# Row maximum on one core: the last rows' pieces cut at multiples of 64 columns, and GpSimd's 38 blocks taken from five loads instead of four

## The chip, the core and the metric

The kernel runs on one core of one Trainium2 chip. The metric is the device time of one execution in microseconds (us). The kernel before has a median of 163.62 us over three timed runs (163.60, 163.62 and 163.85).

The core has several engines that work side by side and wait for each other through semaphores. DVE (VectorE) does the reductions here, PE (TensorE) transposes, ACT (ScalarE) copies PSUM to SBUF, POOL (GpSimd) takes a maximum across partitions, and SP (SyncE) issues the loads. PSUM is the memory that TensorE writes to; SBUF is the main on-chip memory of 128 partitions.

## The reference

```python
def setup_inputs():
    batch, seq, dim = 32, 512, 1024
    return {"x": np.random.randn(batch, seq, dim).astype(np.float32)}

def reference(x):
    return np.max(x, axis=-1).astype(np.float32)
```

There are 32 x 512 = 16384 rows of 1024 float32, so 64 MiB are read and 64 KiB written. Each partition holds 128 rows.

## The kernel before

**Loads.** `BLOCKS` gives the sizes of 18 loads, numbered 0 to 17, in rows per partition: 2, 15, 16, 14, 11, 11, 10, 10, 8, 8, 7, 3, 3, 3, 2, 1, 1, 1. They go into a ring of 47 rows per partition, all from SP's queue (L238). The last two rows of each partition come after them in four smaller transfers, the pieces (L243): `PIECES` holds the widths. `issue()` sends a load as soon as the program has put down the readers of what the load overwrites.

**The plan.** `PLAN` is written out by hand, and `in_turn` keeps each engine's instructions in its order. Its steps are:

- `dN` (`direct`): DVE reduces those rows of load N that it alone handles, into the result columns.
- `tN` (`turn`): GpSimd's share, chunk N. TensorE transposes 128x128 blocks into PSUM (L160), ScalarE copies them to SBUF (L166), GpSimd takes the maximum over the 128 partitions (L168), so one transposed block's row maxima end up side by side in one partition.
- `bN` (`back`): TensorE turns that chunk's results back into a column per block, one small matmul for each block (L178), written into a PSUM tile.
- `pN` (`partial`): where GpSimd has only a part of a row's eight blocks, DVE reduces the rest of the row into a column of the same PSUM tile.
- `mN` (`merge`): DVE reduces the columns of that PSUM tile into the result. `m10` does load 10's tile, called `got`; `m99` does the tile `joint`, which the loads of `RANK` have in common.
- `fN`: DVE reduces piece N. The second piece of a row takes the first one's maximum along as one more column.

**GpSimd's share.** `SHARED = {load: (rows, blocks of each row)}` gives GpSimd 3 rows x 8 blocks of load 10, 2 x 3 of load 13, 2 x 3 of load 14 and 1 x 2 of load 17: 38 blocks in chunks of 8, 8, 8, 6, 6 and 2, which are t0 to t5. The three whole rows of load 10 need nothing of DVE but `m10`.

**What sets the order at the end.** The plan ends `... b1 d13 t3 p13 b2 p14 t4 m10 d15 b3 d16 p17 t5 f0 b4 f1 f2 b5 f3 m99`. A DVE instruction that writes `joint` waits for the TensorE writes to `joint` ahead of it in the plan, and the other way round, since both engines write to one tile. Thus in the kernel before `p17` waits for `b3`, and `b4` waits for `p17`. A DVE write to `joint` also waits for the DVE write to `joint` just ahead of it. The pools `turned` (ACT's copies) and `allr` (GpSimd's results) have two buffers each, so a chunk reuses the buffers of the chunk two ahead of it: GpSimd may write chunk k's result once `b(k-2)` has read the earlier one.

**The end.** Two stores carry the result out from ScalarE's queue: the first block's 112 columns behind `f0` (L271), the second block's 16 columns behind `m99` (L273).

Of the kernel before, what the change touches and what calls it, by code (L numbers as in the profile page):

```python
# [8 lines left out]
F32 = mybir.dt.float32  # L9

BLOCKS = [
    [2, 15, 16, 14, 11, 11, 10, 10, 8, 8, 7],
    [3, 3, 3, 2, 1, 1, 1],
# [1 line left out]
RING = 47  # L17


SHARED = {10: (3, 8), 13: (2, 3), 14: (2, 3), 17: (1, 2)}  # L20

RANK = {13: 1, 14: 2, 17: 2}

PIECES = [(532, 492), (592, 432)]

PLAN = """
    d0 d1 d2 d3 d4 d5 d6 d7 d8 d9 t0 d10 t1 t2 d11 b0 d12 b1 d13 t3 p13 b2 p14 t4 m10 d15 b3
    d16 p17 t5 f0 b4 f1 f2 b5 f3 m99
""".split()

NOSYNC = mybir.DependencyInfo(mybir.DependencyClass.NoSync, mybir.DependencyReason.DATA)
# [4 lines left out]
def kernel(  # L41
# [11 lines left out]
    N, D = xf.shape  # L53
    C = D // P
    I = N // P
# [10 lines left out]
    ring = once.tile([P, I + RING * D], F32)  # L66
    res = ring[:, :I]
# [9 lines left out]
    def maximum(out, in_):  # L77
        return in_turn("DVE", nc.vector.reduce_max(out=out, in_=in_, axis=X))  # L78
# [15 lines left out]

    loads = []
    views = []
    last = len(PIECES)
    first = at = 0
    for sizes in BLOCKS:
        S = sum(sizes) + last * (sizes is BLOCKS[-1])  # L100
        xb = xf[first * P:(first + S) * P, :].rearrange("(p i) d -> p i d", p=P)
# [5 lines left out]
        b, place = 0, {}  # L107
        for i in sorted(range(len(sizes)), key=lambda i: RANK.get(base + i, 0)):
            place[i] = b
# [8 lines left out]
    assert first == I  # L118
    shared = [SHARED.get(j, (0, C)) for j in range(len(loads))]

    lead = [0 if RANK.get(j) == 3 else n - m for j, ((_, n, _, _), (m, _)) in enumerate(zip(loads, shared))]
    final = [j for j in range(len(loads)) if j in RANK]
    final.sort(key=lambda j: loads[j][3])
# [11 lines left out]
    def rows(j):  # L135
        start, n, _, _ = loads[j]
        return ring[:, I + start * D:I + (start + n) * D].rearrange("p (i d) -> p i d", d=D)
# [4 lines left out]
    def share(j):  # L142
        m, parts = shared[j]
        if j in RANK:
            r = loads[j][3] + lead[j] - col0
            return joint[:, r:r + m, :]
        if j not in fetched:
            got = psmall.tile([P, m, parts + (parts < C)], F32)
            fetched[j] = got
        return fetched[j]  # L150
# [39 lines left out]
    def partial(j):  # L190
        m, parts = shared[j]

        s = width - parts if j in RANK else 1
        maximum(share(j)[:, :, parts:], rows(j)[:, lead[j]:lead[j] + m, parts * P:].rearrange(
# [11 lines left out]
    pieces = []  # L206
    tail = []
    room = I + at * D
    for q in range(len(PIECES[0])):
        for r, widths in enumerate(PIECES):  # L210
            c, w = sum(widths[:q]), widths[q]
            room = -(-(room + 1) // 16) * 16
            pieces.append((ring[:, room:room + w], xb[:, S - last + r, c:c + w]))
            if q:
                tail[-last] = (ring[:, room - 1:room], tail[-last][1])
            tail.append((res[:, I - last + r:I - last + r + 1],
                         ring[:, room - (q > 0):room + w]))
            room += w
    assert room <= I + (at + last + 1) * D


# [81 lines left out]
```

## Time and profile before

| what | value |
|---|---|
| median of three timed runs | 163.62 us |
| span of the profiled execution, first to last instruction | 162.0 us |
| what lies around the span, taken as the difference of the two | 1.6 us |
| DVE busy | 135.3 us (84%), 33 instructions |
| POOL busy | 16.0 us (10%) |
| PE busy | 13.6 us (8%) |
| loads | 67.11 MB, mean 415 GB/s over the span |

The profiled execution's own time is not listed apart from the three timed runs, so its span plus 1.6 us stands for it. GpSimd works in the last 20 us of the span alone: the page's slices show POOL idle until load 10 has landed. A row of a group or of the timeline reads: start, duration, engine, line, operation, output<-input, shapes, count, and in brackets how long the engine sat idle before it and what ended that.

### The profile page before, as it was taken

What the parts mean: (1) busy time and instruction counts of PE and PEld (TensorE: products, weight loads), DVE (VectorE), ACT (ScalarE), POOL (GpSimd) and SP (SyncE); (2) the same over time, 40 slices, a digit from 0 to 9 for tenths busy, and PEclk for the clock granted to TensorE, in tenths of its full rate; (3) what the DMA queues carried; (4) which work ended last, traced back from release to release, by engine and by line L of the source; (5) the groups of instructions that cost most, each with busy time, mean ns of one, the idle gap of its engine ahead of it and who ended that gap; (6) DMA issues with size and microseconds to landing.
All of it is one profiled execution on the core that took longest, in us unless ns stands there. A gap on an engine that the chain in (4) does not pass through costs nothing.

```text
span 162.0 us, 297 instructions
## 1 busy us (share of the span) xinstructions
PE 13.6 (8%) x76; PEld 11.7 (7%) x76; DVE 135.3 (84%) x33; ACT 6.3 (4%) x7; POOL 16.0 (10%) x11
## 2 busy tenths in 40 slices
PE   0000000000000000000000000000000000772942
PEld 0000000000000000000000000000000000762731
DVE  3500019998399999999999999996999999999994
ACT  0020000000000000000000000000000000241120
POOL 0000000000000000000000000000000000099791
PEclk9999999999999999999999999999999999997555
DMA  5996999599789999898999899799999999999991
GB/s 176 569 486 273 455 502 518 259 518 518 326 354 453 453 405 534 356 534 356 434 456 455 354 486 465 344 486 388 429 478 388 424 418 453 395 431 419 412 386 47
DMA packets 3456, 67.18 MB, mean 415 GB/s; under 512 B 640, under 2 KB 896, under 8 KB 1536
## 3 DMA queue, kind: packets, MB, share of 16 engines
q1 hardware_dynamic: 3168, 67.11, 97.0%
q10 hardware_dynamic: 288, 0.07, 0.2%
HBM read 67.11 MB, written 0.07 MB: 415 GB/s over the span
## 4 chain that ended last, share of the span: by engine, by line
DMA 50%; DVE 47%; SPq 1%; issue 0%; DVEq 0%
DMA ring<-in_x_dram 50%; DVE ring L78 45%; DVE joint L78 2%; SPq L238 1%; DVEq L298 0%
## 5 line engine op out<-in xcount | busy, mean ns | idle before, releaser
L78 DVE TENSOR_REDUCE ring<-ring 128x1 f32<-128x1024 f32 (+13 forms) x20 | 130.0, 6548 | 23.4 <-DMA ring<-in_x_dram 23.3
L168 POOL PARTITION_ALL_REDUCE top<-sb x6 | 15.7, 2657 | 135.0 <-ACT sb L166 134.9
L160 PE MATMUL ps<-ident,ring 128*128 128x128 f32 x38 | 9.1, 424 | 139.9 <-DMA ring<-in_x_dram 139.9
L160 PEld LDWEIGHTS ps<-ident,ring 128*128 128x128 f32 x38 | 7.6, 224 | 139.9 <-issue 139.9
L166 ACT COPY sb<-ps 128x1024 f32<-128x1024 f32 (+2 forms) x6 | 5.0, 834 | 143.2 <-PE ps L160 136.2
L78 DVE TENSOR_REDUCE joint<-ring 128x2 f32<-128x1280 f32 (+1 forms) x3 | 3.9, 1314 | 0.0
L178 PE MATMUL got<-ident,top 1*128 1x1 f32 x24 | 2.7, 228 | 3.7 <-POOL top L168 3.6
L178 PEld LDWEIGHTS got<-ident,top 1*128 1x128 f32 x24 | 2.4, 188 | 4.6 <-POOL top L168 4.6
L178 PE MATMUL joint<-ident,top 1*128 1x1 f32 x14 | 2.0, 245 | 1.9 <-POOL top L168 1.9
L178 PEld LDWEIGHTS joint<-ident,top 1*128 1x128 f32 x14 | 1.7, 210 | 2.7 <-POOL top L168 2.7
L166 ACT ACT_TABLE_LOAD x1 | 1.3, 1283 | 7.9 <-DVE ring L78 7.9
L83 DVE MEMSET ident<- 128x128 f32 x1 | 0.2, 165 | 0.8 <-PEq L287 0.8
L255 POOL MEMSET gate<- 128x1 f32 x1 | 0.1, 99 | 7.4 <-DVE ring L78 7.4
L90 DVE TENSOR_SCALAR rowno<-rowno 32x1 f32<-32x1 f32 x3 | 0.4, 146 | 0.1
L85 DVE TENSOR_TENSOR_SCAN colno<-ident 128x128 f32<-128x128 f32 x1 | 0.4, 424 | 0.0
L92 DVE TENSOR_SCALAR ident<-colno,rowno 128x128 f32<-128x128 f32 x1 | 0.3, 288 | 0.0
L87 DVE STREAM_TRANSPOSE rowno<-colno 128x32 f32<-128x32 f32 x1 | 0.2, 213 | 0.0
L78 DVE TENSOR_REDUCE ring<-got 128x3 f32<-128x24 f32 x1 | 0.2, 173 | 0.0
L78 DVE TENSOR_REDUCE ring<-joint 128x5 f32<-128x20 f32 x1 | 0.2, 169 | 0.0
L287 POOL MEMSET const-float32-0.0<- 128x1 f32 x1 | 0.1, 98 | 0.2 <-issue 0.2
L287 POOL MEMSET const-bfloat16-1.0<- 128x1 bf16 x1 | 0.1, 101 | 0.0
L287 POOL MEMSET const-uint8-127<- 128x1 uint8 x1 | 0.1, 101 | 0.0
(2 smaller groups left out, 0.2 us busy)
## 6 DMA issues: line engine op xcount, KB each, us to landing
ring<-in_x_dram SPq DMA_DIRECT2D x2, 5632.0 KB, 29.9
ring<-in_x_dram SPq DMA_DIRECT2D x2, 5120.0 KB, 36.8
ring<-in_x_dram SPq DMA_DIRECT2D x2, 4096.0 KB, 32.5
ring<-in_x_dram SPq DMA_DIRECT2D x1, 7680.0 KB, 22.5
ring<-in_x_dram SPq DMA_DIRECT2D x1, 7168.0 KB, 57.8
ring<-in_x_dram SPq DMA_DIRECT2D x3, 1536.0 KB, 35.7
ring<-in_x_dram SPq DMA_DIRECT2D x1, 3584.0 KB, 29.2
ring<-in_x_dram SPq DMA_DIRECT2D x2, 1024.0 KB, 17.7
```

The lines of the kernel that those rows point to most:

```text
L78: return in_turn("DVE", nc.vector.reduce_max(out=out, in_=in_, axis=X))
L83: in_turn("DVE", nc.vector.memset(ident, 1.0))
L85: in_turn("DVE", nc.vector.tensor_tensor_scan(out=colno, data0=ident, data1=ident, initial=-1.0, op0=ALU.add, op1=ALU.mult))
L87: in_turn("DVE", nc.vector.transpose(out=rowno, in_=colno[:, :32]))
L90: in_turn("DVE", nc.vector.tensor_scalar(out=part, in0=part, scalar1=float(q * 32), scalar2=None, op0=ALU.add))
L92: identity = in_turn("DVE", nc.vector.tensor_scalar(out=ident, in0=colno, scalar1=rowno[:, 0:1], scalar2=None, op0=ALU.is_equal))
L160: in_turn("PE", nc.tensor.transpose(out=ps[:, w:w + P], in_=rows(j)[:, lead[j] + r + i, c * P:(c + 1) * P], identity=ident,))
L166: in_turn("ACT", nc.scalar.copy(out=sb[:, :W], in_=ps[:, :W]))
L168: in_turn("POOL", nc.gpsimd.partition_all_reduce(top[:, :W], sb[:, :W], P, bass_isa.ReduceOp.max))
L178: in_turn("PE", nc.tensor.transpose(out=share(j)[:, r + i, c:c + 1], in_=tops[k][0:1, w:w + P], identity=ident[0:1, 0:1],))
L238: load = nc.sync.dma_start(out=rows(issued), in_=src)
L287: nc = _bacc.Bacc("TRN2", target_bir_lowering=False, num_devices=1)
```

## The change

The four pieces of the last two rows become 640 and 384 columns of the one row and 576 and 448 of the other, in the same order of rows; before they were 532 and 492, and 592 and 432. Their places in the source are now multiples of 64 columns, and in the ring they start at multiples of 64 columns instead of 16.

GpSimd's 38 blocks now come from five loads: 6 rows x 4 blocks of load 10, 3 x 2 of load 13, 2 x 2 of load 14, 1 x 2 of load 16 and 1 x 2 of load 17. The chunks are 8, 8, 8, 6, 4, 2 and 2 blocks: t0 to t6, with b0 to b6. DVE takes the rest of these rows in `p10`, `p13`, `p14`, `p16` and `p17`; `d13` and `d16` are gone. `joint` has seven rows of three columns instead of five of four, and `m10` reduces 6 x 5 instead of 3 x 8. The number and the sizes of the 18 loads stay; with load 16 in `RANK`, some loads of the second block take other rows of the source.

```diff
-SHARED = {10: (3, 8), 13: (2, 3), 14: (2, 3), 17: (1, 2)}
-RANK = {13: 1, 14: 2, 17: 2}
-PIECES = [(532, 492), (592, 432)]
+SHARED = {10: (6, 4), 13: (3, 2), 14: (2, 2), 16: (1, 2), 17: (1, 2)}
+RANK = {13: 1, 14: 2, 16: 2, 17: 2}
+PIECES = [(0, 640), (1, 576), (0, 384), (1, 448)]
 PLAN = """
-    d0 d1 d2 d3 d4 d5 d6 d7 d8 d9 t0 d10 t1 t2 d11 b0 d12 b1 d13 t3 p13 b2 p14 t4 m10 d15 b3
-    d16 p17 t5 f0 b4 f1 f2 b5 f3 m99
+    d0 d1 d2 d3 d4 d5 d6 d7 d8 d9 t0 d10 p10 t1 t2 d11 b0 d12 b1 p13 t3 b2 p14 t4 m10 d15 b3
+    p16 t5 p17 t6 b4 f0 f1 b5 f2 f3 b6 m99
 """.split()
...
-    last = len(PIECES)
+    last = 1 + max(r for r, _ in PIECES)
...
-    for q in range(len(PIECES[0])):
-        for r, widths in enumerate(PIECES):
-            c, w = sum(widths[:q]), widths[q]
-            room = -(-(room + 1) // 16) * 16
-            pieces.append((ring[:, room:room + w], xb[:, S - last + r, c:c + w]))
-            if q:
-                tail[-last] = (ring[:, room - 1:room], tail[-last][1])
-            tail.append((res[:, I - last + r:I - last + r + 1],
-                         ring[:, room - (q > 0):room + w]))
-            room += w
+    done = [0] * last
+    before = [None] * last
+    for r, w in PIECES:
+        c, q = done[r], before[r]
+        room = -(-(room + 1) // 64) * 64
+        pieces.append((ring[:, room:room + w], xb[:, S - last + r, c:c + w]))
+        if q is not None:
+            tail[q] = (ring[:, room - 1:room], tail[q][1])
+        before[r] = len(tail)
+        tail.append((res[:, I - last + r:I - last + r + 1], ring[:, room - (q is not None):room + w]))
+        done[r] = c + w
+        room += w
```

More of the change, by code (lines that the diff above doesn't have):

```diff
@@ L208 @@
     room = I + at * D
-    for q in range(len(PIECES[0])):
-        for r, widths in enumerate(PIECES):
-            c, w = sum(widths[:q]), widths[q]
-            room = -(-(room + 1) // 16) * 16
-            pieces.append((ring[:, room:room + w], xb[:, S - last + r, c:c + w]))
-            if q:
-                tail[-last] = (ring[:, room - 1:room], tail[-last][1])
-            tail.append((res[:, I - last + r:I - last + r + 1],
-                         ring[:, room - (q > 0):room + w]))
-            room += w
+    done = [0] * last
[10 more added lines that the diff above has]
+        room += w
+    assert done == [D] * last
     assert room <= I + (at + last + 1) * D
```

## The prediction

> **What bounds the kernel now.** I read the waits first, then the chain that ended last, then the timeline of the last 13 us, engine by engine in short windows so that single instructions show. The waits of DVE, in the rows of the page by shape:
>
> ```profile
> L78 DVE TENSOR_REDUCE ring<-ring 128x15 f32<-128x15360 f32 x1 | 16.2, 16155 | 15.8 <-DMA ring<-in_x_dram 15.8
> L78 DVE TENSOR_REDUCE ring<-ring 128x16 f32<-128x16384 f32 x1 | 17.2, 17222 | 3.2 <-DMA ring<-in_x_dram 3.2
> L78 DVE TENSOR_REDUCE ring<-ring 128x10 f32<-128x10240 f32 x2 | 21.6, 10821 | 1.3 <-DMA ring<-in_x_dram 1.3
> ```
>
> These are DVE's large waits, all for loads, the last ahead of the second 10-row load at 110.82 us. From there DVE has no large gap. The loads come at one pace to the end: issue time plus time to landing in the view of DMA issues gives 149.81 (load 13), 152.3 (14), 154.85 (16), 156.1 (17), and 158.9 for the last piece (149.82 + 9.1). So near the end loads and DVE run level: load 13 lands at 149.81 and DVE, just done with load 12, starts on it at 149.83. The chain in order of time, from there:
>
> ```profile
> 149.83 1.22 DVE ring L78
> 151.05 1.41 DVE joint L78
> 152.46 0.02 issue
> 152.48 1.50 DVE joint L78
> 153.98 2.23 DVE ring L78 x3
> 156.21 0.04 issue
> 156.26 0.96 DVE joint L78
> 157.22 1.16 DVE ring L78 x2
> ...
> 159.00 0.59 DVE ring L78
> ```
>
> Everything here is DVE; whatever it waits for in this stretch moves the end one to one. Now TensorE and GpSimd beside it:
>
> ```profile
> 149.94 1.51 PE L160 MATMUL ps<-ident,ring 128*128 128x128 f32 x6 [0.55 <-DMA ring<-in_x_dram]
> 154.99 0.79 PE L178 MATMUL joint<-ident,top 1*128 1x1 f32 x6 [0.92 <-POOL top L168]
> 157.61 0.79 PE L178 MATMUL joint<-ident,top 1*128 1x1 f32 x6 [0.68 <-POOL top L168]
> 158.66 0.37 PE L178 MATMUL joint<-ident,top 1*128 1x1 f32 x2 [0.25 <-POOL top L168]
> 148.23 3.30 POOL L168 PARTITION_ALL_REDUCE top<-sb  x1
> 152.43 2.50 POOL L168 PARTITION_ALL_REDUCE top<-sb  x1 [0.90 <-ACT sb L166]
> 157.49 1.12 POOL L168 PARTITION_ALL_REDUCE top<-sb  x1
> ```
>
> The second row is `b3`: it begins 0.05 after `t3`'s all-reduce (152.43 to 154.94) and ends at 155.78. In the kernel before only `p17` waits for it, and `p17` starts at 156.26 for load 17's sake. So `b3` is 0.48 us early and shows in no wait. The last small matmuls end at 159.03, 0.48 ahead of `m99` at 159.51.
>
> **Part 1, load 10: no cost.** One reduction of 4096 columns (4.41 us) becomes `d10` of 1024 and `p10` of 3072. A 1024 row takes 1.21 and a 3072 row 3.34, but consecutive reductions overlap: 3072 to 3072 is 146.44 - 143.18 = 3.26 from start to start, 1024 to 1024 is 155.10 - 153.98 = 1.12, and 4096 is 143.18 - 138.85 = 4.33. So the new pair costs 1.12 + 3.26 - 4.33 = 0.05. `p10` reads with a stride and writes to PSUM; the nearest rows (1280 columns, two strided rows to PSUM, 1.48 against 1.33 at 0.96 columns/ns) show the same fixed 0.15 as the contiguous ones, so bounds are -0.05 (no extra) and +0.1. Its cover is the slack at 149.83: load 12's reduction could have been followed at 149.70 and waited for load 13. If that cover is gone, the rest falls into the stall of part 3. TensorE's first three chunks have 24 blocks as before, start with load 10's landing (138.7) as before, and GpSimd's first three all-reduces end at 151.53 as before. `b0` now waits for `p10` too, which ends near 143.3, while `b0` waits for GpSimd until 145.18. `m10` over 30 columns instead of 24: 6 columns, 0.01.
>
> **Part 2, loads 13 to 15.** Before, DVE goes 149.83 to 155.10 with `d13`, `p13`, `p14`, `m10` and `d15`. After: `p13` has 3 x 768 = 2304 columns, 2.40 + 0.15 = 2.55, to 152.38; `p14` waits for its predecessor (0.03, as 152.45 to 152.48 now), 1536 columns, 1.60 + 0.16 = 1.76, to 154.18; `m10` and `d15` follow at the old distances (153.89, 153.98 against `p14`'s end 153.98), so `d15` starts at 154.18 and DVE could go on at 154.18 + 1.12 = 155.30. Against 155.10 that is 0.20 more, for the 256 columns more that lie ahead of this point (the `d16` and `p17` before are 1792 columns, `p16` and `p17` after 1536). The total of columns from load 13 on is equal.
>
> **Part 3, the wait that decides.** `p16` writes `joint` and stands behind `b3` in the plan. In the built program it waits for TensorE's 64th counted matmul: 24 of t0 to t2, 24 of b0 to b2, 6 of t3, 4 of t4, 6 of b3. `b3` does not move: `t3` has six blocks as before, starts from load 13's landing, copies at 151.54, reduces at 152.43, and `b3`'s six matmuls again end at 155.78. (`b3` also waits for `p14`, at 154.18, before GpSimd is done.) TensorE to another engine costs 0.03 to 0.09 (copies: 140.77 to 140.80; 151.45 to 151.54); I take 0.05, since `p16`'s other waits are over by then. So `p16` starts at 155.83, not at 155.30: a stall of 0.53. Behind it on DVE stand `p17`, all four pieces and `m99`, and nothing hides it.
>
> **Part 4, from `p16` to the end on DVE.** `p16` is 768 columns, 0.96; `p17` waits for its end (0.03): 156.82. Then, by the old start-to-start distances and 1/0.96 ns a column: `p17` to `f0` 0.86 (156.26 to 157.12), 157.68; `f0` 0.62 + 108 columns (0.11), 158.41; `f1` 0.68 - 0.02, 159.07; `f2` 0.58 - 0.11, 159.54; `f3` 0.51 + 0.02, so `m99` could start at 160.07. The pieces themselves have landed: the bytes are the same, the last lands near 158.9, and `f3` starts 0.65 later. Their alignment is therefore worth nothing here, whatever it does to a transfer.
>
> **Part 5, the new last round of GpSimd.** `t6` uses `t4`'s result buffer, so it waits for `b4`, which stands behind `t6` on TensorE and waits for `p17` (the last DVE write to `joint`), done at 157.78. `b4` starts 0.05 (GpSimd to TensorE, 154.94 to 154.99) to 0.13 (landing to TensorE, 149.81 to 149.94) later: 157.87. Four matmuls, between two (0.37) and six (0.79): 0.58, to 158.45. GpSimd 0.09 later (as 152.34 to 152.43), 158.54. A 256 all-reduce is 1.12, of which 0.07 overlapped its predecessor: 1.05 to 1.12, to 159.63. `b6` 0.05 + 0.37, 160.05; `m99` 0.05 behind: 160.10. The chunks ahead do not hold `t6`: `t4` of four blocks (512) lies between 1.12 and 2.50, about 1.8, 154.9 to 156.7; `t5` to about 158.0.
>
> Both chains bring `m99` to 160.1, against 159.51: **+0.6**. Its reduction (0.17) and the store are as before; the first store, behind `f0`, is issued 0.7 later and lands 1.6 after that at 160.1, still ahead of the last. The profiled span is 162.0 with 1.6 around it to the median of 163.62, so the forecast is 162.6 + 1.6 = 164.2. Adding the low ends (release 0.03, `t6` 1.05) gives +0.54, the high ends (release 0.09, `b4` 0.13, 1.12) +0.75.
>
> **The rivals.** *The faster clock.* The windows view grants TensorE 1.00 until 147.5 and 0.50 from 147.7 on, and the small matmuls show it: eight of `b0` took 0.65, eight of `b2` 1.01. Had the clock been full at 155, `b3` would take about 0.5 instead of 0.79 and `p16` come 0.28 earlier: +0.3, 163.9. Against it: TensorE does the same work until 152.5, so the clock should fall at the same place. [...] I give this 0.12.
>
> *No stall at all.* The mechanism would be that `b3` is done by 155.30. GpSimd would have to reduce `t3` 0.5 us sooner; it sat idle 0.90 ahead of it, so there is room, but the copy came straight from transposes that wait for load 13. Then `p16` starts at 155.30, each DVE step follows 0.53 earlier, and `m99` is at 159.54 by DVE and 159.6 by part 5: +0.05, 163.65, not slower. The aligned pieces could add to this: two full rows take 2 x 1.28 us to land and the four pieces 2.74 together, so at most 0.18, but DVE reaches `f3` no sooner. [...] Chance 0.08.
>
> *GpSimd's last round is longer.* A start from idle, or a later release of `b4`, adds 0.2 to part 5: `m99` at 160.3 to 160.5, +0.8 to +1.0, 164.4 to 164.6. Against it are GpSimd rows that agree to 0.1. Chance 0.08.
>
> **How the numbers follow.** The forecast holds 0.72. The three timed runs spread by 0.25, so its own range is 164.05 to 164.4; the faster clock takes the low end to 163.8, the long last round the high end to 164.6, and what is left out is no stall and surprises. A difference under 0.2% (0.33 us) can't be told from none here. Slower is the forecast and the long round: 0.8. Within: the faster clock and most of no stall: 0.16. Faster: 0.04.
>
> **What would show it.** In the profile after, DVE idle about 0.45 us ahead of the first 768-column reduction into `joint`, ended by TensorE; that reduction's start near 155.85; GpSimd idle about 0.5 ahead of its last all-reduce, ended by TensorE's `b4`; `f3` starting well after its piece landed; `m99` at 160.1. The prediction is wrong if `p16` starts at 155.3, if `b3` ends at another time, or if DVE's idle time moves to load 13.

## The result and the profile after

The changed kernel has a median of 164.35 us over five runs (164.28 to 164.55), the kernel before 163.63 over five runs taken with them (163.60 to 163.85): a ratio of 1.0042, 95% interval 1.0029 to 1.0055, so about 0.7 us slower. The span of the profiled execution grew from 162.0 to 162.6 us.

The waits of DVE in the kernel after, in the rows of the groups by shape:

```profile
L74 DVE TENSOR_REDUCE ring<-ring 128x15 f32<-128x15360 f32 x1 | 16.2, 16154 | 15.9 <-DMA ring<-in_x_dram 15.9
L74 DVE TENSOR_REDUCE ring<-ring 128x16 f32<-128x16384 f32 x1 | 17.2, 17221 | 3.2 <-DMA ring<-in_x_dram 3.2
L74 DVE TENSOR_REDUCE ring<-ring 128x10 f32<-128x10240 f32 x2 | 21.6, 10820 | 1.3 <-DMA ring<-in_x_dram 1.3
L74 DVE TENSOR_REDUCE joint<-ring 128x1 f32<-128x768 f32 x2 | 1.9, 961 | 0.5 <-PE joint L174 0.4
```

The three waits for loads are what they were. The last row is new: DVE waits for TensorE ahead of a 768-column reduction into `joint`. The chain that ended last, in order of time, from load 13's landing on (start, length, what):

```profile
149.88 1.53 PE ps L156 x6
...
152.37 2.51 POOL top L164
154.88 0.04 issue
154.93 0.81 PE joint L174 x6
155.74 0.02 issue
155.76 0.97 DVE joint L74
156.73 0.02 issue
156.76 0.97 DVE joint L74
157.73 0.14 issue
157.87 0.57 PE joint L174 x4
...
159.66 0.04 issue
159.71 0.38 PE joint L174 x2
160.09 0.02 issue
160.11 0.18 DVE ring L74
```

Before, this stretch was DVE alone. Now it runs through `t3` (TensorE, GpSimd), `b3`, `p16`, `p17`, `b4`, the last all-reduce and `b6` to `m99`. The timeline rows of the two waits, the one on DVE and the one on GpSimd:

```profile
155.76 0.96 DVE L74 TENSOR_REDUCE joint<-ring 128x1 f32<-128x768 f32 x1 [0.42 <-PE joint L174]
158.59 1.06 POOL L164 PARTITION_ALL_REDUCE top<-sb  x1 [0.63 <-PE joint L174]
```

DVE is idle 0.42 us before `p16`. From `p14` to `f3`, a reduction here that waits for nothing starts 0.08 to 0.09 before the one ahead of it ends, and that overlap is lost too, so `p16` starts 0.51 later than it could. GpSimd is idle 0.63 us before `t6`, until `b4` has read the buffer that `t6` overwrites.

Because load 13's landing moves by some tenths between executions (DVE's first reduction of its rows starts at 149.65 to 150.08 us, in e3 and e4 behind a wait for the load of 0.32 and 0.25 us), I compare the profiles by the time from DVE's first reduction of load 13's rows to the start of the last merge. Both starts stand in each timeline:

| profile | first of load 13 | last merge | between |
|---|---|---|---|
| before | 149.83 | 159.51 | 9.68 |
| after | 149.77 | 160.11 | 10.34 |
| e1, `joint` in two tiles | 149.65 | 159.44 | 9.79 |
| e2, own buffers for `t5`, `t6` | 149.68 | 159.91 | 10.23 |
| e3, before + new pieces | 150.08 | 159.75 | 9.67 |
| e4, after + old pieces | 149.98 | 160.32 | 10.34 |
| e5, after, `b3` twice | 149.88 | 160.87 | 10.99 |
| e6, before, `b3` twice | 149.90 | 159.78 | 9.88 |
| e7, after + dummy transposes | 149.90 | 160.24 | 10.34 |
| e8, before, `p13` first + new pieces | 149.78 | 159.46 | 9.68 |

The change costs 0.66 us by this measure, close to the 0.7 of the medians. The measure repeats to 0.01: the kernel before, e3 and e8 give 9.67 to 9.68, and the changed kernel, e4 and e7 give 10.34.

### The profile page after: what moved, and what is told of

The parts are those of the page before. It is cut to its first block, busy times and chain, and to the rows that moved or that the text cites. A ratio compares the mean times of both kernels' runs of the same rounds, so it can differ in the third digit from the quotient of the medians.

```text
span 162.6 us, 303 instructions
## 1 busy us (share of the span) xinstructions
PE 13.3 (8%) x76; PEld 11.3 (7%) x76; DVE 135.5 (83%) x33; ACT 6.4 (4%) x8; POOL 16.3 (10%) x12
## 4 chain that ended last, share of the span: by engine, by line
DMA 49%; DVE 42%; PE 2%; POOL 2%; SPq 1%; POOLq 1%; issue 1%; ACT 0%; ACTq 0%
DMA ring<-in_x_dram 49%; DVE ring L74 41%; POOL top L164 2%; SPq L237 1%; DVE joint L74 1%; PE joint L174 1%; PE ps L156 1%; POOLq L297 1%; ACT sb L162 0%; POOLq L164 0%; ACTq L162 0%
## 5 line engine op out<-in xcount | busy, mean ns | idle before, releaser
L74 DVE TENSOR_REDUCE ring<-ring 128x11 f32<-128x11264 f32 (+12 forms) x18 | 124.5, 6961 | 23.3 <-DMA ring<-in_x_dram 23.3
L162 ACT COPY sb<-ps 128x1024 f32<-128x1024 f32 (+3 forms) x7 | 5.2, 738 | 143.1 <-PE ps L156 141.4
L74 DVE TENSOR_REDUCE joint<-ring 128x1 f32<-128x768 f32 (+2 forms) x4 | 6.2, 1561 | 0.5 <-PE joint L174 0.4
L74 DVE TENSOR_REDUCE got<-ring 128x6 f32<-128x3072 f32 x1 | 3.4, 3351 | 0.0
```

The lines of the kernel that those rows point to most:

```text
L162: in_turn("ACT", nc.scalar.copy(out=sb[:, :W], in_=ps[:, :W]))
```

## The experiments

The theory was that two waits on the tile `joint` cost the time: `p16`'s for `b3`, and the round `p17`, `b4`, `t6`, `b6` behind it. The rivals were that the pieces cost it, that the new split of blocks is simply more work for DVE, and that TensorE's lowered clock makes the difference. The last can be answered from the two traces: the granted clock at `b3` is 0.50 in both, and its six matmuls take 0.79 us before and 0.80 after, so the clock doesn't set the two kernels apart, whatever a full one would be worth. e1 to e4 shared one set of runs of the kernel before (median 163.73 us), e5 to e8 another (163.88), so ratios are compared rather than times.

**e1: take both waits away.** `joint` becomes two tiles; the work stays, and one small merge is added.

```diff
-    joint = pfinal.tile([P, count, width], F32)
+    early = pfinal.tile([P, 5, width], F32)
+    late = pfinal.tile([P, 2, width], F32)
...
-            return joint[:, r:r + m, :]
+            return early[:, r:r + m, :] if r < 5 else late[:, r - 5:r - 5 + m, :]
...
-    p16 t5 p17 t6 b4 f0 f1 b5 f2 f3 b6 m99
+    p16 t5 p17 t6 b4 f0 f1 b5 f2 m98 f3 b6 m99
```

`m98` merges `early`, `m99` merges `late`; the pool `psmall` has two buffers instead of three.

> The changed kernel, with joint split into two PSUM tiles: early for loads 13 and 14, late for 16 and 17, and one more merge of early between f2 and f3. p16 then has no write of TensorE ahead of it in its tile, and b4 no longer waits for p17. If the wait of p16 for b3 and the round behind it are the cause: no idle time of DVE ended by TensorE, p16 at about 155.3 instead of 155.76, b4 near 157, last merge at 159.6 instead of 160.11 (0.09 of it for the additional merge), time 163.7 to 163.85. If DVE's work on the other split of blocks is the cause (rival): 164.35 or 0.1 more, since the work is the same.

Measured: 163.80 us, ratio to before 1.0001 (0.9993 to 1.0010). The timeline of e1, `p16`, then `b4` on TensorE, then the last two all-reduces and the last merge:

```profile
155.13 0.95 DVE L74 TENSOR_REDUCE late<-ring 128x1 f32<-128x768 f32 x1
156.68 0.58 PE L175 MATMUL early<-ident,top 1*128 1x1 f32 x4
156.78 2.11 POOL L165 PARTITION_ALL_REDUCE top<-sb  x2 [0.26 <-ACT sb L163]
159.44 0.15 DVE L74 TENSOR_REDUCE ring<-late 128x2 f32<-128x6 f32 x1
```

`p16` has no bracket, so DVE came to it without idling; `b4` follows straight on `t6`'s transposes, 1.1 us earlier than in the changed kernel when both are counted from load 13's first reduction, and the two all-reduces run back to back. The same blocks in the same chunks, without the waits, are as fast as the kernel before. That rules out the work of the new split as the cause.

**e2: take away the wait of `t6` alone.** `t5` and `t6` get result buffers of their own.

```diff
+    small = ctx.enter_context(tc.tile_pool(name="small", bufs=2))
...
-        top = allr.tile([P, D], F32)
+        if k > 4:
+            top = small.tile([P, 2 * P], F32)
+        else:
+            top = allr.tile([P, D], F32)
```

> The changed kernel, with result buffers of their own for t5 and t6, so that t6's all-reduce doesn't wait until b4 has read t4's buffer; the wait of p16 stays. If both chains reach the last merge at nearly the same time: t6's all-reduce starts right behind t5's, at 157.9 instead of 158.59, but the last merge comes only when f3 is done, 160.0 instead of 160.11: 164.2 to 164.3, 0.1 less. If GpSimd's last round alone sets the end (rival): the last merge at 159.4 to 159.6 and 163.7 to 163.9.

Measured: 164.28 us, ratio 1.0032 (1.0019 to 1.0044). The rows of e2 for `p16`, the last two all-reduces, `b6` and the last merge:

```profile
155.68 0.96 DVE L75 TENSOR_REDUCE joint<-ring 128x1 f32<-128x768 f32 x1 [0.43 <-PE joint L178]
156.81 2.11 POOL L168 PARTITION_ALL_REDUCE top<-sb  x2 [0.26 <-ACT sb L163]
158.97 0.37 PE L178 MATMUL joint<-ident,top 1*128 1x1 f32 x2 [0.43 <-POOL top L168]
159.91 0.17 DVE L75 TENSOR_REDUCE ring<-joint 128x7 f32<-128x21 f32 x1
```

`b6` now ends at 159.34, 0.6 ahead of the merge, yet the merge comes only 0.11 sooner (10.23 against 10.34), because DVE's own chain from the late `p16` is nearly as long. Of the 0.66 us, 0.55 are left when only `p16`'s wait is left, and 0.11 come through GpSimd's round. e1 took away both and gained 0.55 in spite of its additional merge (0.08, from 158.84 to 158.92), that is 0.63 of the 0.66 without it, so the two experiments agree. The 0.11 rests on the profiles; the medians can't show it, since the interval of the ratio overlaps that of the changed kernel.

**e3 and e4: the two halves of the change apart.** e3 puts the new pieces into the kernel before:

```diff
-PIECES = [(532, 492), (592, 432)]
+PIECES = [(640, 384), (576, 448)]
...
-            room = -(-(room + 1) // 16) * 16
+            room = -(-(room + 1) // 64) * 64
```

> The kernel before, with the new pieces alone (640, 576, 384, 448 columns in that order, ring places at multiples of 64). If the pieces are worth nothing: DVE reaches f3 by its own work, the last piece lands 0.05 to 0.1 us earlier behind load 17 than before (2.65 instead of 2.74 us), the last merge at 159.5, time 163.6 to 163.7. If the pieces cost what was lost (rival): 164.3. If their alignment gains: under 163.5.

Measured: 163.74 us, ratio 1.0001 (0.9992 to 1.0010). e4 puts the old pieces into the changed kernel:

```diff
-PIECES = [(0, 640), (1, 576), (0, 384), (1, 448)]
+PIECES = [(0, 532), (1, 592), (0, 492), (1, 432)]
...
-        room = -(-(room + 1) // 64) * 64
+        room = -(-(room + 1) // 16) * 16
```

> The changed kernel, with the old pieces (532, 592, 492, 432 columns, ring places at multiples of 16), so the new split of GpSimd's blocks alone. If the waits on joint are the whole cause: 164.3 to 164.45, p16 again late by 0.4 to 0.5 us for TensorE, b4 behind p17. If the pieces are the cause (rival): 163.6 to 163.8.

Measured: 164.46 us, ratio 1.0039 (1.0025 to 1.0053), with the wait of `p16` as in the changed kernel:

```profile
155.97 0.96 DVE L74 TENSOR_REDUCE joint<-ring 128x1 f32<-128x768 f32 x1 [0.43 <-PE joint L174]
```

The split of the blocks carries the whole loss, the pieces none of it. They gain nothing either, as DVE reaches the last one late: in e3 that piece has landed at 159.05, and `f3` starts at 159.22. In the trace's records of landings the last piece does land sooner behind load 17: 2.65 to 2.68 us in the seven profiles with the new pieces, 2.71 to 2.74 in the three with the old ones. Widths and alignment changed together, so these runs don't say which of them does it.

**e5 and e6: the same dose in both kernels.** `b3`'s six small matmuls are done twice, which ends `b3` about 0.65 us later. The edit is the same in both:

```diff
-        for i in range(q):
+        for i in [*range(q)] * (2 if k == 3 else 1):
```

> The changed kernel, with b3's six small matmuls done twice (same values to the same place), which ends b3 six times 0.108 = 0.65 us later. If p16's wait for b3 is on the path with nothing to cover it: DVE's idle time before p16 grows from 0.42 to 1.05 and all behind it shifts, also b4 and t6; last merge at 160.75, time 165.0. If the wait were covered by something later (rival): less than 0.2 more than the changed kernel.

> The kernel before, with b3's six small matmuls done twice. There only p17 waits for b3, which ends 0.48 us before p17 starts for load 17's sake. If that slack is what the change used up: of 0.65 us 0.15 to 0.25 come through, p17 at 156.45 instead of 156.26, time 163.8 to 163.95. If TensorE's or GpSimd's time at the end counts in any case (rival): 0.65 more, 164.3.

Measured: e5 165.22 us, ratio 1.0085 (1.0071 to 1.0098); e6 164.02 us, ratio 1.0011 (1.0002 to 1.0021). The doubled `b3` and the reduction behind it, from the timeline of e5 and then from the chain that ended last of e6:

```profile
155.05 1.43 PE L174 MATMUL joint<-ident,top 1*128 1x1 f32 x12 [1.36 <-POOL top L164]
156.52 0.96 DVE L74 TENSOR_REDUCE joint<-ring 128x1 f32<-128x768 f32 x1 [1.06 <-PE joint L174]
```

```profile
155.06 1.45 PE joint L178 x12
156.51 0.02 issue
156.53 0.96 DVE joint L78
157.49 0.97 DVE ring L78 x2
```

In the changed kernel DVE's idle time grows from 0.42 to 1.06 and the end moves by 0.65 (10.99 against 10.34): one to one, with no slack. In the kernel before 0.20 of the same delay come through (9.88 against 9.68), and only now does `b3` stand in its chain. The difference, 0.45, is the slack that `b3` had there, read beforehand as 0.48.

**e7: try to keep TensorE's clock up.** Ten transposes of the identity matrix into a spare PSUM tile behind `b0`, two behind `b1`. As in e1, `psmall` has two buffers instead of three.

```diff
-    d0 d1 d2 d3 d4 d5 d6 d7 d8 d9 t0 d10 p10 t1 t2 d11 b0 d12 b1 p13 t3 b2 p14 t4 m10 d15 b3
+    d0 d1 d2 d3 d4 d5 d6 d7 d8 d9 t0 d10 p10 t1 t2 d11 b0 w10 d12 b1 w2 p13 t3 b2 p14 t4 m10 d15 b3
...
+    def warm(n):
+        for _ in range(n):
+            in_turn("PE", nc.tensor.transpose(out=spare, in_=ident, identity=ident))
```

> The changed kernel, with 10 transposes of the identity into a spare PSUM tile behind b0 and 2 behind b1, to keep TensorE busy so that its granted clock may stay at 1.00 beyond 147.5 us. If the clock stays up until b3: b3's six matmuls take 0.5 instead of 0.80 and t3's transposes may be shorter too, p16 comes 0.3 to 0.5 us earlier and b4 and b6 are shorter, time 163.8 to 164.05. If the clock falls as before: no change, 164.35, or up to 0.1 more where the additional transposes hold up b1 or t3.

Measured: 164.80 us, ratio 1.0059 (1.0045 to 1.0072). The view by stretches of e7 (stretch, length; busy time and count of PE, PEld, DVE, ACT, POOL; granted clock, DMA share, GB/s):

```profile
142.30:145.60 3.30, 1.39 (x16) 1.15 (x14) 3.30 (x2) 1.39 (x2) 3.30 (x2) 1.00 1.01 425
145.70:149.00 3.30, 3.15 (x19) 2.73 (x18) 3.30 (x2) 0.54 (x1) 3.30 (x2) 0.50 1.00 423
154.90:156.00 1.10, 0.94 (x7) 0.93 (x8) 0.68 (x2) 0.00 (x0) 1.10 (x2) 0.50 1.01 396
```

The clock fell to 0.50 ahead of the dummies and stayed there through a stretch in which TensorE was busy 3.15 of 3.30 us. `b3` took 0.79 as before, and the stretch from load 13 to the last merge is the same 10.34. So this experiment failed to make the condition that it was to test: what a full clock at 155 us would be worth was not measured. Nor did the time stay within the 0.1 us more that was expected for a clock that falls: the ratio is 0.0017 above the changed kernel's, some 0.3 us. That lies outside the span: in the profiled execution 2.06 us lie around it, instead of 1.77 to 1.81 in the other eight profiled executions whose time is listed, and all four timed runs of e7 have 2.0 to 2.1. Why the twelve matmuls, or what else e7 changes, lengthen that part stays open.

**e8: does the kernel before have a wait to gain from?** There `p14` waits for the write of `p13` just ahead of it. e8 puts `d13`, which writes elsewhere, between them, and takes the new pieces as in e3.

```diff
-    d0 d1 d2 d3 d4 d5 d6 d7 d8 d9 t0 d10 t1 t2 d11 b0 d12 b1 d13 t3 p13 b2 p14 t4 m10 d15 b3
+    d0 d1 d2 d3 d4 d5 d6 d7 d8 d9 t0 d10 t1 t2 d11 b0 d12 b1 p13 t3 d13 b2 p14 t4 m10 d15 b3
```

> The kernel before, with p13 put ahead of d13, so that p14 doesn't stand right behind the write to joint that it waits for, and with the new pieces. p14's wait for p13 (0.03 us idle, and the overlap of 0.09 that is lost with it) goes; DVE is at d15 0.1 earlier. If DVE's work alone sets the end: the last merge at 159.4 and 163.55. If load 17's landing at 156.1 sets p17's start in any case: the last merge at 159.5, no difference, 163.6 to 163.7.

Measured: 163.82 us, ratio 0.9997 (0.9988 to 1.0006). From the timeline of e8, `p13`, `d13`, `p14`, then `p17` and the last merge, and below them TensorE's transposes of load 17:

```profile
149.78 1.50 DVE L78 TENSOR_REDUCE joint<-ring 128x2 f32<-128x1280 f32 x1
151.18 1.21 DVE L78 TENSOR_REDUCE ring<-ring 128x1 f32<-128x1024 f32 x1
152.34 1.50 DVE L78 TENSOR_REDUCE joint<-ring 128x2 f32<-128x1280 f32 x1
...
156.21 0.96 DVE L78 TENSOR_REDUCE joint<-ring 128x2 f32<-128x768 f32 x1
...
159.46 0.17 DVE L78 TENSOR_REDUCE ring<-joint 128x5 f32<-128x20 f32 x1
...
156.23 0.66 PE L160 MATMUL ps<-ident,ring 128*128 128x128 f32 x2 [0.49 <-DMA ring<-in_x_dram]
```

`p14` starts 2.56 us behind load 13's first reduction, where before it took 2.65 to the same point (149.83 to 152.48). The 0.09 is gone again by `p17`, which starts 6.43 behind that first reduction in both kernels: load 17 lands at 156.09, TensorE's transposes wait for it until 156.23, and `p17` starts with them at 156.21, some 0.1 later than DVE's own work would let it. No version here beats the kernel before by anything that can be measured.

## Why the prediction was right

The time was forecast as 164.2 us, from 163.8 to 164.6, and slower; it is 164.35.

- **Load 10, forecast at no cost.** Right. From the first reduction of load 10 to that of load 11 it is 4.39 us instead of 4.33, where 0.05 more was forecast; `p10` took 3.35 (3.26 to the next start). The slack ahead of load 13 covered it, and DVE went on to load 13 at its landing without a gap.
- **Loads 13 to 15, 0.20 us more on DVE up to `p16`.** Right: `d15` started 4.36 behind `p13`'s start, forecast 4.35.
- **`p16` held by `b3`, 0.53 us.** Right: 0.51, and `b3` took 0.80 and ended at 155.73 where 155.78 was forecast. e1 and e5 show that this wait has no cover, e6 that it had 0.45 us of it before.
- **DVE from `p16` to the end.** `f3` could have been followed at 160.0; forecast 160.07 from a `p16` 0.07 later. Right.
- **GpSimd's last round, `m99` at 160.10.** Right in its steps: `m99` started at 160.11, released by `b6`, and `t6` ran 1.06 us, within the 1.05 to 1.12 given. But `b4`'s release took 0.14 (157.73 to 157.87), just past the high end of 0.05 to 0.13, and from `b4`'s end to `t6` it was 0.16 (158.43 to 158.59) instead of 0.09. So this chain brings `m99` 10.34 behind load 13's first reduction, where 10.27 was forecast. That `m99` still stands at 160.11, almost on the forecast's 160.10, is luck in part: load 13's first reduction came 0.06 earlier than in the profile before. e2 shows that this round is worth 0.11 beyond DVE's chain; the forecast had 0.03.
- **The pieces, worth nothing.** Right, by e3 and e4.
- **The median.** The medians differ by 0.72 us, where 0.59 was forecast (159.51 to 160.10). GpSimd's round, mis-sized by the 0.07 just named, is the one part of this that the profiles show; the rest is less than the runs can tell, as the interval of the ratio stands for 0.47 to 0.90 us. What lies around the span was taken as 1.6 us, the profiled span of the kernel before taken from the median of other executions; the profiled executions with both numbers, e7 apart, have 1.77 to 1.81. With 1.78 the profiled execution of the kernel before comes to 163.73, some 0.1 above the median. So the 1.6 is too small, but only because the profiled execution was a little longer than the median one, and it doesn't explain a difference between the kernels.

Of the rivals, no stall and a longer last round did not come. The full clock at `b3` did not come either: the clock's records give a full rate that begins between 142.0 and 144.3 us and lasts 3.41 us in each of the ten profiles. Its start moves by 2.3 us between executions, though TensorE's work begins at 138.6 to 138.9 in all of them. So the same work did not keep the fall at the same place, against the prediction's argument; what sets it these runs don't show, and no run shows a full clock at `b3`, the case that was given 0.12. In all ten the full rate ended by 147.7, some 7 us ahead of `b3`.

## What to carry to other kernels

In this program a PSUM tile that two engines fill in turn makes each write wait for the other engine's earlier ones, even where they touch different columns: in `joint` `p16` waited 0.42 us for `b3` and `b4` 0.99 us for `p17`; in e1 `p16` did not wait, in a tile that `b3` doesn't write. Before moving such a write earlier, look for what stands ahead of it in that tile and when that ends, because the wait with slack appeared in no view of the kernel before. The question for a change at a balanced end is not how much work each engine gets (here it stayed nearly the same: DVE is busy 135.5 us instead of 135.3, GpSimd 16.3 instead of 16.0) but which result now has to be there sooner; 0.48 us of slack turned into 0.51 us of stall. A second tile took the wait away and cost one small merge of 0.08 us.

## What was not expected

A stretch of 3.3 us with TensorE 95% busy did not raise its clock again in e7. Ten of the 19 matmuls in it were full 128x128 transposes, the others small ones. It had risen during the 24 transposes of load 10: in e7 they start 0.21 us apart until 142.1 and 0.11 apart from 142.3 on, just where the trace's record of a full clock begins, so the 1.00 that the view shows ahead of the first record, which the prediction took as granted, is not a full clock. What a stretch must hold to raise the clock these runs don't tell. The new pieces landed 0.03 to 0.09 us sooner behind load 17 than the old ones (2.65 to 2.68 against 2.71 to 2.74), though their widths differ too.
